# Moving the elementwise work of three attentions from GpSimd to VectorE in a two-layer hybrid encoder

## The chip, the cores and the metric

The kernel runs on one core of a Trainium2 chip, in one launch. The metric is the device time of an execution in microseconds; of several executions the median is given. A core has five engines with queues of their own: TensorE (PE, its weight loads PEld), VectorE (DVE), ScalarE (ACT), GpSimd (POOL) and SyncE (SP, which issues the DMAs here). Each works its queue off in order; they wait for each other by semaphores.

## The reference

Two layers (`DEPTH`), 512 tokens, 1024 features, all in float32. In each layer a wide projection feeds three attentions of 8 heads whose gated outputs are added:

```python
h = rms_norm(x, norm_mix[l]);  u = h @ w_in[l]
qa, ka, va, fa, qd, kvd, kr, qc, kc, vc, gl = split(u)
# A: causal, with cumulated log forget gates; q and k normalised per head
ya = prefix_block_attention(rms_norm(qa), rms_norm(ka), va, True, cum_logf)
# B: low rank; q and k of 64 normalised and 32 normalised and rotated columns a head
qb  = rms_norm(qd, mla_q_norm[l]) @ w_q_up[l]
kvb = rms_norm(kvd, mla_kv_norm[l]) @ w_kv_up[l]
q_mla = concat([rms_norm(qb[..., :64]), rope(rms_norm(qb[..., 64:]))])
k_mla = concat([rms_norm(kvb[..., :64]), rope(rms_norm(kr))])
yb = prefix_block_attention(q_mla, k_mla, kvb[..., 64:], False)
# C: chunks, with a clipped relative bias; q and k normalised per head
yc = chunk_band_attention(rms_norm(qc), rms_norm(kc), vc, rel_bias[l])
x = x + sum(sigmoid(gl + b_gate) * (y_n @ w_branch[l, n]) for n in A, B, C) @ w_out[l]
x = x + relu(rms_norm(x, norm_ffn[l]) @ w_ff1[l])**2 @ w_ff2[l]
```

## The kernel before

Every float32 product is made of three matmuls of the rounded form `fp32r`: each operand is split in a high and a low part, and high x high, low x high and high x low are added in PSUM. A weight chunk of 1024 columns comes by DMA into `raw`; ScalarE rounds it to `whi` (L140), VectorE subtracts to get `wlo` (L141). There are three buffers of each, and `take` puts both splits some places ahead of where it is called. Of each step of three matmuls it is the third that reads `wlo`.

The order of TensorE's instructions is written by the program (`manual_schedule` names PE alone). On the other engines a scheduler orders the instructions from their dependencies and priorities, so the order there follows when the data would be ready; what is moved from one engine to another also moves its neighbours.

A layer runs so: `qk_proj` projects A's queries and keys (four token blocks of 128) and normalises them per head: squares and means in `evac`, a reciprocal root by Newton steps (`rsqrt`, L251 to L255), the factor `fqk`, and eight multiplies (L403) over both `tok` tiles. `rotary_key` (L496 to L517) normalises and rotates the shared key. `attention` is a generator that is run step by step between the matmuls of other work (`fill`): scores S, transposed probabilities P (`ptl`, L715), values V, where every second head ends with the scale of the pair (L736), and transposes T of the next heads. Then C in the same way, with `branch(0)` as filler, and then B.

For B a string of letters (`TUNE["mla"]`) sets the order of the matmuls: `d` and `u` are the down projections (`mla_down`, whose evacuation splits the result, L456 and L457, squares it, L459, and adds the squares, L461), `0` and `1` the sums of these squares on TensorE and the factors from them (`mla_factor`: `ps_sum`, L292, then L480 to L483), `q` the queries' up projection (`mla_q`), `k` that of keys and values (`mla_kv`, weights `kvup`), `b` steps of `branch(2)`, `t` the transposes that attention B begins with (`ps_q`, L584), `g` a gate:

```python
mla='ddddddddddddubuubu0qqqbbqqqqqbbuuuubqbbb1kbbktkkkbbbkkkbtbbgg',
```

`mla_q` ends with the norms and rotations of the four token blocks (L568 to L576: six multiplies and adds each), two blocks on VectorE and two on GpSimd:

```python
e = nc.gpsimd if t % 2 else nc.vector
```

`mla_kv` scales the keys in the same way (L541), after `mf`, the factor from `1`, has scaled the projection out of PSUM (L490, L492). `branch` multiplies each gate with the product (L810) and adds it to the merged output (L811), on GpSimd but in the last branch. GpSimd also adds the causal mask (L685), cumulates squares for the layer norms (L284), makes the rotary tables (L235) and copies the rotary key (L530).

Of the kernel before, what the change touches and what calls it, by code (L numbers as in the profile page):

```python
# [13 lines left out]
ALU = mybir.AluOpType  # L14
# [10 lines left out]
H = 8  # L25
HD = 64
NOPE = 64
ROPE = 32
# [44 lines left out]
    head=1.0,  # L73
# [103 lines left out]
class Kern:  # L177
# [201 lines left out]
    def qk_proj(self, l, col, scale, out, tags=("s", "s", "mm", "mm")):  # L379
        nc = self.nc  # L380
        tok = [self.tk("tok", [P, 2, 512], F32) for _ in range(2)]
        out.append(tok)
        ms = self.small(NT * H, "ms", 1)
        ms4 = ms.rearrange("p (t h) -> p t h", h=H)

        def evac(t, ps):
            u = tok[t // 2][:, t % 2]
            nc.scalar.activation(out=u, in_=ps, func=AF.Copy, scale=self.rtok[:, t : t + 1])
            sq = self.tmp()
            nc.scalar.activation(out=sq, in_=ps, func=AF.Square, scale=self.rtok[:, t : t + 1])  # L390
            nc.vector.tensor_reduce(out=ms4[:, t], in_=sq.rearrange("p (h d) -> p h d", d=HD), axis=AX.X, op=ALU.add)

        yield from self.win_group(l, col, evac, tags)
        v = self.small(NT * H, "msv", 1)
        nc.vector.tensor_scalar(out=v, in0=ms, scalar1=1.0 / HD, scalar2=EPS, op0=ALU.mult, op1=ALU.add)
        y = self.rsqrt(v, NT * H)
        f = self.small(NT * H, "fqk")
        nc.vector.tensor_scalar(out=f, in0=y, scalar1=scale, scalar2=None, op0=ALU.mult)
        f4 = f.rearrange("p (t h) -> p t h", h=H)
        for p in range(4):  # L400
            for tp in range(2):
                u = tok[tp][:, :, p * P : (p + 1) * P].rearrange("p t (h d) -> p t h d", d=HD)
                nc.gpsimd.tensor_tensor(out=u, in0=u, in1=f4[:, 2 * tp : 2 * tp + 2, 2 * p : 2 * p + 2].unsqueeze(3).to_broadcast([P, 2, 2, HD]), op=ALU.mult)  # L403

    def v_evac(self, vt, t, ps, sc):
        nc = self.nc
# [89 lines left out]
    def rotary_key(self):  # L496

        nc = self.nc
        ps = self.pt.tile([P, T], F32, tag="pt", name="ps_kr")
        for t in range(NT):  # L500
            nc.tensor.transpose(ps[:, t * ROPE : (t + 1) * ROPE], self.kr[:, t * P : (t + 1) * P], self.ident[0:ROPE, 0:ROPE])
        krt = self.sm.tile([P, NT, ROPE], F32, tag="krt", name="krt", bufs=1)
        nc.vector.tensor_tensor(out=krt, in0=ps[:, 0 : NT * ROPE].rearrange("p (t d) -> p t d", d=ROPE), in1=self.rtok.unsqueeze(2).to_broadcast([P, NT, ROPE]), op=ALU.mult)
        sq = self.tmp()[:, 0 : NT * ROPE].rearrange("p (t d) -> p t d", d=ROPE)
        nc.gpsimd.tensor_tensor(out=sq, in0=krt, in1=krt, op=ALU.mult)
        v = self.small(NT, "krv", 1)
        nc.vector.tensor_reduce(out=v, in_=sq, axis=AX.X, op=ALU.add)
        nc.vector.tensor_scalar(out=v, in0=v, scalar1=1.0 / ROPE, scalar2=EPS, op0=ALU.mult, op1=ALU.add)
        y = self.rsqrt(v, NT)
        tab, hr = self.rtab, ROPE // 2  # L510
        nc.gpsimd.tensor_tensor(out=krt, in0=krt, in1=y.unsqueeze(2).to_broadcast([P, NT, ROPE]), op=ALU.mult)
        sw = self.tmp()[:, 0 : NT * ROPE].rearrange("p (t d) -> p t d", d=ROPE)
        for c in range(2):
            nc.gpsimd.tensor_tensor(out=sw[:, :, c * hr : (c + 1) * hr], in0=krt[:, :, (1 - c) * hr : (2 - c) * hr], in1=tab[:, 3, :, c * hr : (c + 1) * hr], op=ALU.mult)
        nc.gpsimd.tensor_tensor(out=krt, in0=krt, in1=tab[:, 2], op=ALU.mult)
        nc.gpsimd.tensor_tensor(out=krt, in0=krt, in1=sw, op=ALU.add)
        self.krt = krt  # L517

    def mla_kv(self, l, state):
# [17 lines left out]
        for t in range(NT):  # L537
            tp, tt = divmod(t, 2)
            u = kt[tp][:, tt, :, 0:NOPE]
            e = nc.gpsimd if t % 2 else nc.vector  # L540
            e.tensor_tensor(out=u, in0=u, in1=y4[:, t].unsqueeze(2).to_broadcast([P, H, NOPE]), op=ALU.mult)  # L541
        yield from group(1, lambda t, ps: self.v_evac(vt, t, ps, f))

    def mla_q(self, l, state):
# [18 lines left out]
        tab, hr = self.rtab, ROPE // 2  # L563
        for t in range(NT):
            tp, tt = divmod(t, 2)
            e = nc.gpsimd if t % 2 else nc.vector
            u = qt[tp][:, tt, :, 0:NOPE]
            e.tensor_tensor(out=u, in0=u, in1=fq4[:, t, 0].unsqueeze(2).to_broadcast([P, H, NOPE]), op=ALU.mult)  # L568
            u = qt[tp][:, tt, :, NOPE:KB]
# [53 lines left out]
    def attention(self, l, branch, fill_ns, qkv):  # L623
# [94 lines left out]
        def values(h, gi, x):  # L718
# [14 lines left out]
            r0 = HD * (h % 2)  # L733
            nc.vector.tensor_tensor(out=y[r0 : r0 + HD], in0=yps[0:HD], in1=half[0:HD], op=ALU.add)
            if h % 2 == 1:
                (nc.gpsimd if h + 1 < H else nc.vector).tensor_tensor(out=y, in0=y, in1=head[h]["scale"], op=ALU.mult)  # L736
                a, b = self.ypool.tile([P, T], F32R, tag="yh", name="yh", bufs=4), self.ypool.tile([P, T], F32R, tag="yl", name="yl", bufs=4)
                nc.scalar.activation(out=a, in_=y, func=AF.Copy)
                nc.vector.tensor_tensor(out=b, in0=y, in1=a.bitcast(F32), op=ALU.subtract)
# [44 lines left out]
    def branch(self, l, n, y, done=None, pool=None):  # L784

        nc = self.nc
        for m in range(0, KT, 2):
# [10 lines left out]
            for u, k in order:  # L798
# [5 lines left out]
                if k == 3:  # L804
# [326 lines left out]
```

## Time and profile before

| what | value |
|---|---|
| median of 3 executions | 1841.53 us (1840.97 to 1844.39) |
| the profiled execution, its own time | 1842.65 us |
| its span, first to last instruction | 1840.9 us |
| mean granted TensorE clock | 0.996 |
| TensorE busy | 1808.0 us, 98% |
| VectorE busy | 1056.5 us, 57% |
| ScalarE busy | 784.6 us, 43% |
| GpSimd busy | 216.7 us, 12% (257 instructions) |

A row of a timeline gives the start in the span, the time taken, the engine, line and operation, what it writes and reads by the program's names, the shapes, and in brackets the idle time before it and what ended that. A matmul's end is modelled, so its length overlaps the next one's: matmuls of 512 columns start 0.23 us apart at full clock and are given 0.39 each. A wait of TensorE's is therefore read from the starts. Lengths on the other engines are measured, also with a small overlap of neighbours that do not depend on each other.

### The profile page before, as it was taken

The numbers are of one execution on the slowest core, as the hardware profiler recorded it, in microseconds if no ns is written. First come the engines' busy times: TensorE is split into PE (matmuls) and PEld (weight loads), VectorE is DVE, ScalarE is ACT, GpSimd is POOL, SyncE is SP. The second block draws the span as 40 slices with busy tenths as digits, with TensorE's granted clock in tenths as the row PEclk, the third lists the DMA queues.
The fourth block names the chain that finished last, engine by engine and source line by source line (L and its number), as shares of the span: only waits on it lengthen the run. The fifth ranks groups of instructions, "written<-read, shape, count | busy, mean of one in ns | idle before, by whom it ended". The sixth has DMA issues, their size and how long they took to land.

```text
span 1840.9 us, 23250 instructions
## 1 busy us (share of the span) xinstructions
PE 1808.0 (98%) x8496; PEld 1489.7 (81%) x8496; DVE 1056.5 (57%) x1994; ACT 784.6 (43%) x1369; POOL 216.7 (12%) x257
## 2 busy tenths in 40 slices
PE   8999999989999999999999999999899999999999
PEld 6888888868888888888888788888688888888887
DVE  7565477497765632553355654765977655325531
ACT  6565456446643222222245644664366432212311
POOL 1321200150011000000123202001500110000000
PEclk9999999999999999999999999999999999999999
DMA  5564365322353333333345633653234433333331
GB/s 179 157 167 122 104 182 143 121 94 87 114 167 92 94 101 92 93 102 109 109 125 144 172 109 108 185 146 118 86 92 141 135 92 103 93 92 97 97 115 58
DMA packets 84226, 217.85 MB, mean 118 GB/s; under 512 B 13696, under 2 KB 16768, under 8 KB 84112
## 3 DMA queue, kind: packets, MB, share of 16 engines
q1 hardware_dynamic: 84112, 216.37, 40.3%
q8 instruction: 67, 1.10, 0.2%
q14 instruction: 47, 0.39, 0.1%
HBM read 178.44 MB, written 12.71 MB: 104 GB/s over the span
## 4 chain that ended last, share of the span: by engine, by line
PE 87%; DVE 6%; ACT 3%; DMA 2%; issue 1%; SPq 1%; POOL 0%; DVEq 0%; ACTq 0%; POOLq 0%
PE ps L332 38%; PE ps_f L332 14%; PE ps_t L367 14%; PE ps_o L332 5%; PE ps_b L802 5%; PE ps_s L682 3%; PE ps_y L725 3%; PE ps_p L712 2%; PE ps_q L584 1%; DVE wlo L141 1%; SPq L599 1%; ACT whi L140 1%; DMA kl<-nat 1%; DMA cb<-cum 0%; PE ps_k L349 0%
## 5 line engine op out<-in xcount | busy, mean ns | idle before, releaser
L140 ACT ACTIVATE whi<-raw 128x1024 fp32r<-128x1024 f32 (+1 forms) x337 | 307.3, 919 | 771.8 <-issue 316.0
L141 DVE TENSOR_TENSOR wlo<-raw,whi 128x1024 fp32r<-128x1024 f32 (+1 forms) x337 | 358.9, 1069 | 253.2 <-ACT whi L140 237.6
L332 PE MATMUL ps<-ah,wlo 128*128 128x512 f32 x512 | 201.7, 394 | 0.0
L332 PE MATMUL ps<-ah,whi 128*128 128x512 f32 x512 | 201.7, 394 | 0.0
L332 PE MATMUL ps<-al,whi 128*128 128x512 f32 x512 | 201.7, 394 | 0.0
L332 PE MATMUL ps<-xgh,whi 128*128 128x512 f32 x512 | 199.4, 390 | 0.0
L332 PE MATMUL ps<-xgl,whi 128*128 128x512 f32 x512 | 199.2, 389 | 0.0
L332 PE MATMUL ps<-xgh,wlo 128*128 128x512 f32 x512 | 199.2, 389 | 0.0
L332 PE MATMUL ps_f<-xgh,whi 128*128 128x512 f32 x464 | 195.9, 422 | 0.0
L332 PE MATMUL ps_f<-xgh,wlo 128*128 128x512 f32 x464 | 182.5, 393 | 0.0
L332 PE MATMUL ps_f<-xgl,whi 128*128 128x512 f32 x464 | 182.1, 393 | 0.0
L367 PE MATMUL ps_t<-whi,xgh 128*128 128x512 f32 x384 | 151.4, 394 | 6.7 <-ACT whi L140 6.7
L367 PE MATMUL ps_t<-whi,xgl 128*128 128x512 f32 x384 | 150.2, 391 | 0.0
L367 PE MATMUL ps_t<-wlo,xgh 128*128 128x512 f32 x384 | 150.2, 391 | 0.0
L332 PEld LDWEIGHTS ps<-al,whi 128*128 128x128 f32 x512 | 95.7, 187 | 23.7
L332 PEld LDWEIGHTS ps<-ah,wlo 128*128 128x128 f32 x512 | 95.7, 187 | 23.7
L332 PEld LDWEIGHTS ps<-ah,whi 128*128 128x128 f32 x512 | 95.7, 187 | 23.7
L332 PEld LDWEIGHTS ps<-xgh,wlo 128*128 128x128 f32 x512 | 96.1, 188 | 20.1
L332 PEld LDWEIGHTS ps<-xgl,whi 128*128 128x128 f32 x512 | 96.1, 188 | 20.0
L332 PEld LDWEIGHTS ps<-xgh,whi 128*128 128x128 f32 x512 | 96.1, 188 | 19.9
L715 DVE TENSOR_TENSOR ptl<-ps_p,pth 128x512 fp32r<-128x512 f32 x144 | 85.9, 599 | 43.7 <-ACT pth L714 42.6
L956 DVE SCALAR_TENSOR_TENSOR t<-ps,rb 128x512 f32<-128x512 f32 x64 | 43.9, 691 | 114.2 <-PE ps L332 111.6
(196 smaller groups left out, 3202.8 us busy)
## 6 DMA issues: line engine op xcount, KB each, us to landing
raw<-w SPq DMA_DIRECT2D x277, 512.0 KB
qq<-nat SPq DMA_DIRECT2D x64, 128.0 KB
kk<-nat SPq DMA_DIRECT2D x64, 128.0 KB
kl<-nat SPq DMA_DIRECT2D x64, 128.0 KB
gd<-t SPq DMA_DIRECT2D x32, 256.0 KB
t<-rows SPq DMA_DIRECT2D x48, 128.0 KB
cb<-cum SPq DMA_DIRECT2D x16, 256.0 KB
cb<-gd SPq DMA_DIRECT2D x16, 256.0 KB
```

The lines of the kernel that those rows point to most:

```text
L140: nc.scalar.activation(out=hi[:, c : c + v], in_=raw[:, c : c + v], func=AF.Copy)
L141: nc.vector.tensor_tensor(out=lo[:, c : c + v], in0=raw[:, c : c + v], in1=hi[:, c : c + v].bitcast(F32), op=ALU.subtract)
L332: nc.tensor.matmul(out=ps, lhsT=a[:, k], rhs=b[k], start=first and k == 0 and j == 0, stop=last and k == n - 1 and j == 2)
L367: nc.tensor.matmul(out=pss[t][:, 0:width], lhsT=a[k][:, t * P : t * P + P], rhs=b[:, i], start=c == 0 and i == 0 and j == 0, stop=last and ...
L584: nc.tensor.transpose(ps[0:rows, t * P : (t + 1) * P], src(t), self.ident)
L599: nc.sync.dma_start(out=s[rows, u].bitcast(F32), in_=x[own].bitcast(F32))
L682: nc.tensor.matmul(out=ps[:, 0:n], lhsT=a[:, i * P : (i + 1) * P], rhs=b[:, 0:n], start=j == 0, stop=j == len(terms) - 1)
L712: nc.tensor.transpose(ps[:, o + (i - kb) * P : o + (i - kb + 1) * P], pr[:, offs[i] + kb * P : offs[i] + (kb + 1) * P], self.ident)
L715: nc.vector.tensor_tensor(out=pl[:, 0:w], in0=ps[:, 0:w], in1=ph[:, 0:w].bitcast(F32), op=ALU.subtract)
L725: nc.tensor.matmul(out=yps[:, kb * P : T], lhsT=qkv[2][kb // 2][:, kb % 2, h, :], rhs=head[h][gi][x][:, o : o + T - kb * P], start=gi == 0 ...
L802: nc.tensor.matmul(out=pss[u], lhsT=chunk[a][:, u, k], rhs=y[b][k], start=k == 0 and j == 0, stop=k == 3 and j == 2)
L956: nc.vector.scalar_tensor_tensor(out=t, in0=ps, scalar=0.0, in1=self.rb, op0=ALU.max, op1=ALU.mult)
```

## The change

Seven places in the attentions and in `branch` issue on VectorE what GpSimd did: the norms (L403), the rotary key (L505 to L516), the odd token blocks of B's keys (L541) and queries (L568 to L576), the scale of a pair (L736) and the addition of a gated product (L811). In the changed kernel lines behind 540 count one less.

```diff
-                nc.gpsimd.tensor_tensor(out=u, in0=u, in1=f4[:, 2 * tp : 2 * tp + 2, 2 * p : 2 * p + 2]
...
+                nc.vector.tensor_tensor(out=u, in0=u, in1=f4[:, 2 * tp : 2 * tp + 2, 2 * p : 2 * p + 2]
...
-        nc.gpsimd.tensor_tensor(out=sq, in0=krt, in1=krt, op=ALU.mult)
+        nc.vector.tensor_tensor(out=sq, in0=krt, in1=krt, op=ALU.mult)
...
-        nc.gpsimd.tensor_tensor(out=krt, in0=krt, in1=sw, op=ALU.add)
+        nc.vector.tensor_tensor(out=krt, in0=krt, in1=sw, op=ALU.add)
...
-            e = nc.gpsimd if t % 2 else nc.vector
-            e.tensor_tensor(out=u, in0=u, in1=y4[:, t].unsqueeze(2).to_broadcast([P, H, NOPE]), op=ALU.mult)
+            nc.vector.tensor_tensor(out=u, in0=u, in1=y4[:, t].unsqueeze(2).to_broadcast([P, H, NOPE]), op=ALU.mult)
...
-            e = nc.gpsimd if t % 2 else nc.vector
+            e = nc.vector
...
-                (nc.gpsimd if h + 1 < H else nc.vector).tensor_tensor(out=y, in0=y, in1=head[h]["scale"], op=ALU.mult)
+                nc.vector.tensor_tensor(out=y, in0=y, in1=head[h]["scale"], op=ALU.mult)
...
-                        (nc.vector if done else nc.gpsimd).tensor_tensor(out=s, in0=s, in1=g, op=ALU.add)
+                        nc.vector.tensor_tensor(out=s, in0=s, in1=g, op=ALU.add)
```

The order on TensorE is the same. GpSimd keeps 48 rows in its queue's listing, which had 130. On VectorE the order changes at each of the places. The first one is in layer 0, in branch B, at the end of `mla_q`: VectorE's queue from the split of the last down projection (L457; `st`) over the sum of its squares (L461; `pr`) to the mean behind the sums (L480). Before:

```order
L457 SCALAR_TENSOR_TENSOR st<-ps_f,vec,st 128x512
L575 TENSOR_TENSOR tok<-tok,rtab 128x8x32
L573 TENSOR_TENSOR t_3957<-tok,rtab 128x8x16
L576 TENSOR_TENSOR tok<-tok,t_3943 128x8x32
L461 TENSOR_TENSOR pr<-pr 128x512
L573 TENSOR_TENSOR t_3957<-tok,rtab 128x8x16
L141 TENSOR_TENSOR wlo<-raw,whi 128x1024
L575 TENSOR_TENSOR tok<-tok,rtab 128x8x32
L810 SCALAR_TENSOR_TENSOR cb<-cb,ps_b 128x512
L480 SCALAR_TENSOR_TENSOR mv_4005<-ps_sum,r_4006 128x4
```

The L141 in it splits the first weights of `kvup`. In the changed kernel (lines one less, so L575 is L574 there):

```order
L457 SCALAR_TENSOR_TENSOR st<-ps_f,vec,st 128x512
L572 TENSOR_TENSOR t_3943<-tok,rtab 128x8x16
L569 TENSOR_TENSOR tok<-tok,fqv 128x8x32
L574 TENSOR_TENSOR tok<-tok,rtab 128x8x32
L461 TENSOR_TENSOR pr<-pr 128x512
L575 TENSOR_TENSOR tok<-tok,t_3943 128x8x32
L572 TENSOR_TENSOR t_3950<-tok,rtab 128x8x16 x2
L567 TENSOR_TENSOR tok<-tok,fqv 128x8x64
L574 TENSOR_TENSOR tok<-tok,rtab 128x8x32
L569 TENSOR_TENSOR tok<-tok,fqv 128x8x32
L480 SCALAR_TENSOR_TENSOR mv_4005<-ps_sum,r_4006 128x4
```

Four rotations stand ahead of L457 now (L567, L569, L567, L572) where six stood, and L141 is no longer between L461 and L480. It stands behind nine more rotations and the small steps of the factor:

```order
L575 TENSOR_TENSOR tok<-tok,t_3957 128x8x32
L254 SCALAR_TENSOR_TENSOR rs_t_4012<-rs_t_4012,mv_4005 128x4
L572 TENSOR_TENSOR t_3964<-tok,rtab 128x8x16
L255 SCALAR_TENSOR_TENSOR rs_y_4011<-rs_t_4012,rs_y_4011 128x4
L572 TENSOR_TENSOR t_3964<-tok,rtab 128x8x16
L253 TENSOR_TENSOR rs_t_4012<-rs_y_4011 128x4
L141 TENSOR_TENSOR wlo<-raw,whi 128x1024
L254 SCALAR_TENSOR_TENSOR rs_t_4012<-rs_t_4012,mv_4005 128x4
L574 TENSOR_TENSOR tok<-tok,rtab 128x8x32
L255 SCALAR_TENSOR_TENSOR rs_y_4011<-rs_t_4012,rs_y_4011 128x4
L809 SCALAR_TENSOR_TENSOR cb<-cb,ps_b 128x512
L483 TENSOR_TENSOR mf_4007<-rs_y_4011,rtok 128x4
```

Of the 24 rotations 22 are ahead of this L141; the factor `mf` (L483) comes soon behind it.

The second place is in attention A of layer 0, where the first pair of heads ends: VectorE's queue from the value sum (L734) to the low part of the output (L739; L738 in the changed kernel). Before:

```order
L734 TENSOR_TENSOR t_1017<-ps_y,t_1163 64x512
L691 ISA pr,mn<-ps_s,cb 128x512
L691 ISA mn 128x1
L715 TENSOR_TENSOR ptl<-ps_p,pth 128x512
L739 TENSOR_TENSOR yl<-t_1017,yh 128x512
```

In the changed kernel:

```order
L733 TENSOR_TENSOR t_1017<-ps_y,t_1163 64x512
L690 ISA pr,mn<-ps_s,cb 128x512
L690 ISA mn 128x1
L735 TENSOR_TENSOR t_1017<-t_1017,t_1105 128x512
L714 TENSOR_TENSOR ptl<-ps_p,pth 128x512
L690 ISA pr,mn<-ps_s,cb 128x384
L690 ISA mn 128x1
L738 TENSOR_TENSOR yl<-t_1017,yh 128x512
```

The scale of the pair (L736, here L735) now stands in VectorE's queue ahead of the low part of the probabilities.

## Rows read from the trace of the kernel before

**Rows 1.** The page, busy time by engine: us, share of the span, instructions.

```profile
PE 1808.0 (98%) x8496; PEld 1489.7 (81%) x8496; DVE 1056.5 (57%) x1994; ACT 784.6 (43%) x1369; POOL 216.7 (12%) x257
```

**Rows 2.** TensorE's waits: waited for; us in total, times, longest us.

```profile
PE ps_sum L292 <- DVE pr L461: 7.8, 2, 3.9
...
PE ps_q L584 <- DVE tok L541: 2.2, 3, 1.0
```

**Rows 3.** Timeline of TensorE at the first wait for the sums.

```profile
381.79 0.40 PE L802 MATMUL ps_b<-yh,wlo 128*128 128x512 f32 x1
386.10 1.87 PE L292 MATMUL ps_sum<-ones,pr 128*128 128x2 f32 x8 [3.91 <-DVE pr L461]
387.83 1.20 PE L367 MATMUL ps_t<-whi,st 128*128 128x512 f32 x2
388.83 0.63 PE L367 MATMUL ps_t<-wlo,st 128*128 128x512 f32 x1
```

**Rows 4.** Stretches: us, busy time of PE, PEld, DVE, ACT, POOL, then granted clock.

```profile
382.00:386.00 4.00, 0.19 (x1) 0.00 (x0) 4.00 (x7) 1.54 (x2) 3.77 (x7) 0.98 0.00 0
386.00:393.00 7.00, 6.90 (x21) 5.79 (x22) 7.00 (x12) 0.00 (x0) 5.26 (x4) 0.52 0.40 113
...
1300.50:1307.50 7.00, 7.00 (x21) 5.71 (x21) 7.00 (x11) 0.00 (x0) 5.27 (x4) 0.51 0.39 114
```

**Rows 5.** Timeline of VectorE in the same place.

```profile
377.27 0.69 DVE L568 TENSOR_TENSOR tok<-tok,fqv 128x512 f32<-128x512 f32 x1
377.88 1.27 DVE L570 TENSOR_TENSOR tok<-tok,fqv 128x256 f32<-128x256 f32 x1
...
382.36 0.74 DVE L457 SCALAR_TENSOR_TENSOR st<-ps_f,vec,st 128x512 fp32r<-128x512 f32 x1
...
385.10 0.94 DVE L461 TENSOR_TENSOR pr<-pr 128x512 f32<-128x512 f32 x1
...
386.70 1.21 DVE L141 TENSOR_TENSOR wlo<-raw,whi 128x1024 fp32r<-128x1024 f32 x1
...
389.37 0.41 DVE L576 TENSOR_TENSOR tok<-tok,t 128x256 f32<-128x256 f32 x1
389.71 1.24 DVE L481 TENSOR_SCALAR mv<-mv 128x4 f32<-128x4 f32 x1
```

**Rows 6.** Timelines of GpSimd (two rows) and ScalarE there.

```profile
377.37 1.50 POOL L568 TENSOR_TENSOR tok<-tok,fqv 128x512 f32<-128x512 f32 x1 [2.75 <-DVE fqv L562]
...
389.46 1.46 POOL L811 TENSOR_TENSOR mg<-mg,cb 128x512 f32<-128x512 f32 x1 [0.96 <-DVE mv L480]
...
383.13 0.60 ACT L459 ACTIVATE pr<-ps_f 128x512 f32<-128x512 f32 x1 [5.10 <-DVE st L457]
```

**Rows 7.** Groups of VectorE's instructions: busy us, mean ns of one, idle before.

```profile
L573 DVE TENSOR_TENSOR t<-tok,rtab 128x128 f32<-128x128 f32 x8 | 6.7, 862 | 0.0
...
L736 DVE TENSOR_TENSOR t<-t,t 128x512 f32<-128x512 f32 x6 | 4.2, 693 | 0.2
...
L507 DVE TENSOR_REDUCE krv<-t 128x4 f32<-128x128 f32 x2 | 0.6, 280 | 0.4 <-POOL t L505 0.4
```

**Rows 8.** Timeline of TensorE, the waits behind the first.

```profile
399.65 0.73 PE L367 MATMUL ps_t<-whi,st 128*128 128x512 f32 x2 [0.59 <-ACT t L492]
...
412.63 0.42 PE L584 MATMUL ps_q<-ident,tok 128*96 128x128 f32 x2 [1.03 <-DVE tok L541]
...
415.81 0.73 PE L682 MATMUL ps_s<-st 96*128 96x512 f32 x2 [1.14 <-DVE st L587]
...
421.90 1.30 PE L682 MATMUL ps_s<-st 96*128 96x512 f32 x3 [0.52 <-DVE mn L691]
```

**Rows 9.** Timeline of VectorE: a pair's end in attention A; a projection of C.

```profile
134.66 0.69 DVE L715 TENSOR_TENSOR ptl<-ps_p,pth 128x512 fp32r<-128x512 f32 x1 [1.04 <-ACT pth L714]
...
205.59 1.23 DVE L141 TENSOR_TENSOR wlo<-raw,whi 128x1024 fp32r<-128x1024 f32 x1 [3.91 <-ACT whi L140]
```

More of the change, by code (lines that the diff above doesn't have):

```diff
@@ L402, in qk_proj @@
                 u = tok[tp][:, :, p * P : (p + 1) * P].rearrange("p t (h d) -> p t h d", d=HD)
-                nc.gpsimd.tensor_tensor(out=u, in0=u, in1=f4[:, 2 * tp : 2 * tp + 2, 2 * p : 2 * p + 2].unsqueeze(3).to_broadcast([P, 2, 2, HD]), op=ALU.mult)
+                nc.vector.tensor_tensor(out=u, in0=u, in1=f4[:, 2 * tp : 2 * tp + 2, 2 * p : 2 * p + 2].unsqueeze(3).to_broadcast([P, 2, 2, HD]), op=ALU.mult)
     def v_evac(self, vt, t, ps, sc):
@@ L510, in rotary_key @@
         tab, hr = self.rtab, ROPE // 2
-        nc.gpsimd.tensor_tensor(out=krt, in0=krt, in1=y.unsqueeze(2).to_broadcast([P, NT, ROPE]), op=ALU.mult)
+        nc.vector.tensor_tensor(out=krt, in0=krt, in1=y.unsqueeze(2).to_broadcast([P, NT, ROPE]), op=ALU.mult)
         sw = self.tmp()[:, 0 : NT * ROPE].rearrange("p (t d) -> p t d", d=ROPE)
         for c in range(2):
-            nc.gpsimd.tensor_tensor(out=sw[:, :, c * hr : (c + 1) * hr], in0=krt[:, :, (1 - c) * hr : (2 - c) * hr], in1=tab[:, 3, :, c * hr : (c + 1) * hr], op=ALU.mult)
-        nc.gpsimd.tensor_tensor(out=krt, in0=krt, in1=tab[:, 2], op=ALU.mult)
-        nc.gpsimd.tensor_tensor(out=krt, in0=krt, in1=sw, op=ALU.add)
+            nc.vector.tensor_tensor(out=sw[:, :, c * hr : (c + 1) * hr], in0=krt[:, :, (1 - c) * hr : (2 - c) * hr], in1=tab[:, 3, :, c * hr : (c + 1) * hr], op=ALU.mult)
+        nc.vector.tensor_tensor(out=krt, in0=krt, in1=tab[:, 2], op=ALU.mult)
+        nc.vector.tensor_tensor(out=krt, in0=krt, in1=sw, op=ALU.add)
         self.krt = krt
```

## The prediction

> **What bounds the kernel now.** I read the busy times first: TensorE is busy for 98% of the span and VectorE for 57% [rows 1]. The change touches no matmul and no matmul's place, so it can move the time only through TensorE's waits, and the second view is the list of those. It is short. Waiting for the sums of squares of the latent keys (`ps_sum`, released by VectorE's L461) takes 7.8 us in two pieces, one in each layer, and waiting for the scaled keys of branch B (L541) 2.2 us in three [rows 2]. The third view is TensorE in order of time at the first of these: its last matmul of `ps_b` starts at 381.79, the eight sums only at 386.10, and the projection `kvup` behind them at 387.83 [rows 3]. The fourth, the stretches with the granted clock, tells what such an idle time costs on top: in 386 to 393 the clock is 0.52 of full, so the 1.2 GHz level held for 0.48 x 7 / 0.5 = 6.7 us, until 392.7; at 1300.5 to 1307.5, in the other layer, it is 0.51 [rows 4]. The fifth shows why VectorE is late there: it runs the rotations of branch B's queries without a pause, and at the same time GpSimd runs the other half of them [rows 5, 6].
>
> These two do not run side by side. L568 of VectorE begins at 377.27 and takes 0.69, L568 of GpSimd begins at 377.37; VectorE's next multiply, on half the elements, takes 1.27 and ends at 379.15, some 0.29 after GpSimd's L568 has let go at 378.87. The same 128x256 size takes 0.41 at 389.37, when GpSimd is idle. L481, which works on four elements a partition, takes 1.24 at 389.71, while GpSimd adds a gate (L811, 1.46 from 389.46) [rows 5, 6]. So a GpSimd operation on two operands holds up a VectorE one that falls into it for nearly its whole length.
>
> **The change, part by part.** Everything is counted per layer; there are two.
>
> *Durations after the move.* 128x512 on VectorE takes 0.69 (L736, six of which are there already), 128x256 takes 0.41 [rows 5, 7]. For 128x128 no free multiply is in the trace; the bounds are the reduction L507 with 0.28 and the contended L573 with 0.86 [rows 7]. I take 0.28, since the two other sizes went back to such values where GpSimd was idle. Independent neighbours overlap by some 0.08 (377.27 + 0.69 against 377.88), so the steps are 0.61, 0.34 and 0.20.
>
> *Rotations (L568 to L576).* VectorE issues 24 instead of 12. Ahead of the split of `kvup`'s weights stand 22 of them now: 4 of 0.61, 10 of 0.34 and 8 of 0.20, 7.4 us together. With 0.86 - 0.28 = 0.58 more for each, as L573 has it, they would take 7.4 + 22 x 0.58 = 20.2, the other bound. The Trainium skill ("SBUF — State Buffer", Who interferes with whom) has it that a VectorE instruction with two SBUF inputs and a GpSimd instruction that reads SBUF exclude each other, whichever starts first. By that rule the free lengths hold once GpSimd has nothing here, as the trace suggests, and the sum stands; by the lengths as they are in the rows it would be the slow rival below. The added gate (L811, 0.61) goes ahead of the reciprocal roots, and one root step that was held for 1.1 is free again, so the first rotation starts at about 376.7 instead of 377.27. In the new order L457 comes behind four rotations (378.5, in place of 382.36) and L461 behind three more. ScalarE's square between them takes 0.60 and starts as L457 ends [rows 6], so L461 runs from 380.0 to 380.7. TensorE comes to the sums at 381.79 + 0.23 = 382.02: **the first wait is gone**, with 1.3 us to spare.
>
> *What is late next.* The eight sums take 0.8, the first two matmuls of `kvup` (which read `whi`) follow at 382.83, and the third reads `wlo`. Its split (L141) was in VectorE's queue behind L461 and one rotation; now it comes behind L461, fifteen rotations and ten small steps of the factor. From 380.6 that is 0.34 + 0.40 + 0.61 + 0.34 + 0.34 to 382.6, the mean (L480) when the sums are in at 383.0, then 3.7 us of rotations and small steps to 386.7, and 1.22 for the split. It ends at 387.9; before, it ended at 386.70 + 1.21 = 387.91 [rows 5]. By coincidence that is the same moment. So TensorE stands from 383.5 to about 387.95, 4.5 us, now at the third matmul of `kvup`, and the wait has changed its place. That third matmul starts 0.86 earlier than at 388.83 [rows 3]. An idle of that size cost the clock before, and I expect the fall again; coming back at 392.7 to 394, it leaves between 0.5 gained and 0.1 lost at the end of this stretch. I take **0.2**.
>
> *The waits behind it.* The factor `mf` (L483) was late because GpSimd's gates held three root steps for 1.1 us each; now it comes at 389.0, and TensorE's wait at 399.65 (idle 0.59; a start-to-start step of 0.23 under a modelled length of 0.39 makes each wait 0.16 longer than its idle) goes: **0.75**. The keys' scales (L541) are four of 0.61 on VectorE where two ran on each engine, but with the factor 9 us earlier they begin as soon as the keys are there, at about 406, and are through at 408.6, while TensorE, with its clock down, is at their transposes at about 410. That wait goes: 2.2 / 2 + 2 x 0.16 = **1.4**. The next one, for the split L587 (415.81, idle 1.14, so 1.3), shrinks to about 0.5, since the queue ahead of L587 stays the same: **0.8**. The one at 421.90 (0.52 + 0.16) goes, since a split held by GpSimd's gate ahead of the scores is free: **0.7** [rows 2, 8].
>
> *Norms (L403, 8 per projection, 64 in all).* They cost VectorE 8 x 0.34 = 2.7 us at each of eight places. VectorE idles 3.9 us between two splits there [rows 9], and with three weight buffers the split behind them is for a chunk that TensorE reads some 5 us later (24 matmuls of 0.23 to a chunk). Nothing, unless that slack is used up; then up to 2.7 a place.
>
> *Scales of the pairs (L736, 18), rotary key, remaining gates (L811).* 18 x 0.61 on VectorE in the softmax stream, ahead of L715. VectorE waits 1.04 for ScalarE at that very point in the second pair [rows 9]: nothing, at most 0.6 each where it does not wait.
>
> **Sum:** 0.2 + 0.75 + 1.4 + 0.8 + 0.7 = 3.85 per layer, 7.7 in all. The profiled execution took 1842.65 (span 1840.9 and 1.75 around it) and would take 1834.95; it stands 1.1 over the median of 1841.53, so the forecast is **1833.8**.
>
> **Rivals.** *The clock stays up.* The idle is now broken by sums and two matmuls. For: the stretch without matmuls of 512 columns shrinks from 5.8 us (382.0 to 387.83) to 4.5. Against: both layers fell, and 4.5 is still long. From 387.95 to 392.7 half of the time comes back, 2.4 in place of 0.2: 1831.6 if in one layer, 1829.4 if in both.
>
> *The long durations are the rotations' own* (broadcast and strided operands), not GpSimd's doing. Then the 22 take 12.8 us longer per layer ahead of the split, TensorE's third matmul comes 12 us later than now, and the later waits stay: about 1841.5 + 24 = 1865. It turns slower once the 22 take over 7.4 + 4.5 us, 0.54 each. Against it stand the 0.41 at 389.37 and the four elements that took 1.24. The Trainium skill ("Perfetto Trace Analysis", Optimizing Scalar/DVE Operations) says that it may pay to move work off a saturated VectorE, even to GpSimd, and that this might not help because they share a port. VectorE is saturated here (4.00 of 4.00 us in 382 to 386 [rows 4]), so the first half of that sentence speaks against the change; the trace bears out the second half.
>
> *The softmax stream pays.* If L736 delays L715 in all of the 18 places, 18 x 0.61 = 11 comes back: 1844.8; in half of them 1839.3. For: TensorE waits in the attentions are all on VectorE and ScalarE. Against: the pause of 1.04.
>
> **How the numbers follow.** Forecast 0.55, clock up in one layer or both 0.25, softmax stream 0.13, own durations or another loss on VectorE 0.07. About 0.2%, 3.7 us, is what a measurement can tell: faster 0.80, same 0.13, slower 0.07. The range goes from a little under the case of full clock in both layers, 1827.5, to 1840.5 in the softmax case.
>
> **What would show it.** Right: no wait at `ps_sum`, a wait of 4 to 5 us at `ps_t` on `wlo` (L141) in each layer, the granted clock near 0.5 for some 6 us behind it, L568 to L576 at 0.69, 0.41 and 0.28, and no wait on the keys' scales. Wrong: L461 still late, rotations over 0.5 on average, or new waits on `ptl` in the attentions.

## The result and the profile after

The changed kernel took **1831.96 us** (median of 6 runs, 1829.80 to 1833.69), the kernel before 1842.05 (6 runs, 1840.89 to 1844.70): a ratio of 0.9943, with an interval of 0.993 to 0.9955. That is 10.1 us, more than the 3.7 that a measurement can tell, 1.8 below the forecast of 1833.8 and inside its range. The profiled executions differ by as much: 1842.65 and 1832.57, spans 1840.9 and 1830.8.

The page's busy times, us, share and instructions (before: [rows 1]):

```profile
PE 1803.2 (98%) x8496; PEld 1489.0 (81%) x8496; DVE 1080.6 (59%) x2132; ACT 783.8 (43%) x1369; POOL 88.8 (5%) x119
```

138 instructions went over. GpSimd lost 127.9 us by it and VectorE gained 24.1, 0.17 for each, less than the shortest of them takes (0.24, the 128x64 multiplies of the rotary key): VectorE's own instructions have become shorter. TensorE's waits (waited for; us, times, longest) [rows 2]:

```profile
PE ps_t L367 <- DVE wlo L141: 8.4, 2, 4.2
...
PE ps_s L681 <- DMA kl<-nat: 3.9, 4, 1.0
PE ps_y L724 <- DVE ptl L714: 1.2, 2, 1.1
...
PE ps_s L681 <- DVE st L586: 0.6, 2, 0.3
```

The sums (`ps_sum`) and the keys (`tok`, L540) are gone from the list; in their place stands one wait a layer for the split of `kvup`'s weights, as foretold. The wait on `ptl` is new; a new wait there was named as a sign of being wrong. Its long piece (1.06) is in attention C of layer 0: VectorE stands 1.08 there for a load of C's queries (`qq`, from 285.88 to 286.96), and its split of `ptl` comes behind. It is not the scale of a pair that holds it. The waits for the loads of `kl` are the same 3.9 in four as before. TensorE in order of time, at the places of [rows 3, 8]:

```profile
382.31 0.40 PE L801 MATMUL ps_b<-yh,wlo 128*128 128x512 f32 x1
382.55 0.95 PE L292 MATMUL ps_sum<-ones,pr 128*128 128x2 f32 x8
383.36 0.71 PE L367 MATMUL ps_t<-whi,st 128*128 128x512 f32 x2
388.29 0.80 PE L367 MATMUL ps_t<-wlo,st 128*128 128x512 f32 x1 [4.22 <-DVE wlo L141]
...
398.81 0.62 PE L367 MATMUL ps_t<-whi,st 128*128 128x512 f32 x2
...
409.91 0.60 PE L583 MATMUL ps_q<-ident,tok 128*96 128x128 f32 x4
```

The sums follow the last matmul of `ps_b` by 0.24 us where it was 4.31. In the windows (us; busy PE, PEld, DVE, ACT, POOL; granted clock; DMA) the idle time still costs the clock, in both layers [rows 4]:

```profile
382.00:386.00 4.00, 2.07 (x14) 1.49 (x12) 3.61 (x16) 0.00 (x0) 0.00 (x0) 1.00 0.00 0
386.00:393.00 7.00, 4.71 (x11) 3.79 (x12) 7.00 (x20) 1.27 (x2) 0.00 (x0) 0.51 0.42 114
...
1294.00:1301.00 7.00, 4.49 (x11) 3.55 (x12) 7.00 (x20) 1.27 (x2) 0.00 (x0) 0.51 0.42 112
```

VectorE there, to be held against [rows 5]: the 128x256 multiply behind the first L567 takes 0.42 and not 1.27, and L481 on four elements 0.17 and not 1.24.

```profile
377.17 0.69 DVE L567 TENSOR_TENSOR tok<-tok,fqv 128x512 f32<-128x512 f32 x1
377.78 0.42 DVE L569 TENSOR_TENSOR tok<-tok,fqv 128x256 f32<-128x256 f32 x1
...
380.45 0.69 DVE L461 TENSOR_TENSOR pr<-pr 128x512 f32<-128x512 f32 x1
...
383.94 0.17 DVE L481 TENSOR_SCALAR mv<-mv 128x4 f32<-128x4 f32 x1
...
387.00 1.23 DVE L141 TENSOR_TENSOR wlo<-raw,whi 128x1024 fp32r<-128x1024 f32 x1
```

By groups (busy us, mean ns, idle before) the durations are those taken in the prediction, the 128x128 multiply's among them, for which only bounds were to be had [rows 7]:

```profile
L567 DVE TENSOR_TENSOR tok<-tok,fqv 128x512 f32<-128x512 f32 x8 | 5.5, 688 | 0.1
...
L572 DVE TENSOR_TENSOR t<-tok,rtab 128x128 f32<-128x128 f32 x16 | 4.4, 286 | 0.0
...
L569 DVE TENSOR_TENSOR tok<-tok,fqv 128x256 f32<-128x256 f32 x8 | 3.4, 421 | 0.0
```

Where the 10.2 us between the last matmuls come from, by the starts of the same matmul in both traces:

| us gained | layer 0 | layer 1 | forecast |
|---|---|---|---|
| sums, split and clock | 0.61 | 0.84 | 0.2 |
| factor (L492) | 0.87 | 0.74 | 0.75 |
| keys' scales (L541) | 1.54 | 1.49 | 1.4 |
| split of the latent keys (L587) | 1.15 | 1.17 | 0.8 |
| last scores (421.90) | 0.56 | 0.52 | 0.7 |
| **branch B** | **4.73** | **4.76** | **3.85** |
| attention A | 0.45 | 0.82 | 0 |
| attention C | -0.76 | 0.27 | 0 |

The program's start takes 0.21 back, and 0.14 lies between the places. Branch B is the result. A second profile of the same changed kernel (after_again, the last experiment) gives 4.60 and 4.04 for it: the first line is 0.51 and 0.25 there, and the others agree within 0.13. So the first line varies by up to 0.6 from one execution to the next. In the attentions these two profiles differ by up to 1.5 us in a stretch, so a sum of that size is not resolved there by one profile of each; single waits are (rest_back below). The -0.76 holds the wait behind the load of C's queries; of the other runs best1 alone shows it, with 1.08.

### The profile page after: what moved, and what is told of

It is laid out like the page before. It is cut to its first block, busy times and chain, and to the rows that moved or that the text cites. A ratio compares the mean times of both kernels' runs of the same rounds, so it can differ in the third digit from the quotient of the medians.

```text
span 1830.8 us, 23198 instructions
## 1 busy us (share of the span) xinstructions
PE 1803.2 (98%) x8496; PEld 1489.0 (81%) x8496; DVE 1080.6 (59%) x2132; ACT 783.8 (43%) x1369; POOL 88.8 (5%) x119
## 4 chain that ended last, share of the span: by engine, by line
PE 94%; DVE 2%; DMA 1%; ACT 1%; SPq 1%; issue 0%; POOL 0%; DVEq 0%; ACTq 0%; POOLq 0%
PE ps L332 39%; PE ps_f L332 17%; PE ps_t L367 16%; PE ps_b L801 7%; PE ps_o L332 5%; PE ps_s L681 4%; PE ps_y L724 3%; PE ps_p L711 3%; PE ps_q L583 1%; SPq L598 1%; DMA kl<-nat 1%; PE ps_k L349 0%; PE ps_sum L292 0%; DMA qq<-nat 0%; ACT whi L140 0%
## 5 line engine op out<-in xcount | busy, mean ns | idle before, releaser
L141 DVE TENSOR_TENSOR wlo<-raw,whi 128x1024 fp32r<-128x1024 f32 (+1 forms) x337 | 353.6, 1053 | 236.0 <-ACT whi L140 220.4
```

What stands on the lines that cost most here:

```text
L141: nc.vector.tensor_tensor(out=lo[:, c : c + v], in0=raw[:, c : c + v], in1=hi[:, c : c + v].bitcast(F32), op=ALU.subtract)
```

## Experiments: undoing one part

Each of these four is the changed kernel with one part of the work on GpSimd again; the fifth is the kernel before with one part moved. "Cost" is how much longer branch B is than in the changed kernel's trace, layer 0 / layer 1. The kernel before took 1843.04 beside these and beside the three that follow them, 1843.43 beside spare and best1, and 1842.37 beside both and after_again.

**rot_back**, half of the rotations on GpSimd again:

```diff
-            e = nc.vector
+            e = nc.gpsimd if t % 2 else nc.vector
```

> The changed kernel with the odd token blocks' rotations (L567 to L575) on GpSimd again, 12 a layer; all else stays on VectorE. My theory (a GpSimd operation with two operands holds VectorE up for its length): VectorE's rotations beside them take 1.27 and 0.86 again in place of 0.42 and 0.28, the latent keys' squares are summed some 5 us later (L461 near 386), TensorE waits 3 to 4 us at the sums in each layer and then once more, 1 to 3 us, at the third matmul of kvup: 2 to 4 us a layer slower than the changed kernel, 1836 to 1840. Rival (the two engines run side by side, GpSimd was only slow and late itself): VectorE has 4 us less to do ahead of the split of kvup, its durations stay at 0.69, 0.42 and 0.28, the wait at kvup goes: about 1822.

Measured: 1836.23 (ratio 0.9957, 0.9944 to 0.9969), cost 1.85 / 3.06. VectorE is held again, and TensorE, in the second fence, waits for the sums:

```profile
375.24 1.27 DVE L569 TENSOR_TENSOR tok<-tok,fqv 128x256 f32<-128x256 f32 x1
376.43 1.10 DVE L567 TENSOR_TENSOR tok<-tok,fqv 128x512 f32<-128x512 f32 x1
377.45 1.13 DVE L572 TENSOR_TENSOR t<-tok,rtab 128x128 f32<-128x128 f32 x1
...
385.08 0.15 DVE L480 SCALAR_TENSOR_TENSOR mv<-ps_sum,r 128x4 f32<-128x4 f32 x1
...
395.11 0.16 DVE L483 TENSOR_TENSOR mf<-rs_y,rtok 128x4 f32<-128x4 f32 x1
```

```profile
382.28 1.86 PE L292 MATMUL ps_sum<-ones,pr 128*128 128x2 f32 x8 [2.11 <-DVE pr L461]
...
397.70 0.73 PE L367 MATMUL ps_t<-whi,st 128*128 128x512 f32 x2 [2.12 <-ACT t L492]
```

The wait for the sums is 2.1, less than before: no addition of GpSimd's holds L251 ahead of the rotations (0.19 here, 1.28 before), and L457 stands behind four of VectorE's rotations and not six. The one for the factor (L492) is 2.12 where it was 0.59 [rows 8]. Both come with the rotations, but the cost does not stand at the sums. Up to the end of the lower clock behind them this run is 0.85 and 1.15 us ahead of the changed kernel, since the wait at the third matmul of `kvup` is gone in layer 0 and 1.3 in layer 1; it loses 2.4 and 4.0 at the factor (in layer 1 the clock falls once more behind it, to 0.50 from 1307.4 to 1310.7). From L480 to L483 it takes 10.03 us here, and no step of the root is longer than 0.17: other work of VectorE's stands between them. Before it took 8.84, in the changed kernel 5.68. So the order of the queue, which the move changes too, makes most of this wait, and not a hold of the root steps.

**gate_back**, the gated additions on GpSimd again but for the last branch's:

```diff
-                        nc.vector.tensor_tensor(out=s, in0=s, in1=g, op=ALU.add)
+                        (nc.vector if done else nc.gpsimd).tensor_tensor(out=s, in0=s, in1=g, op=ALU.add)
```

> The changed kernel with the addition of the gated products (L810) on GpSimd again, 16 places. My theory: an addition of 1.46 there holds small steps of the reciprocal root and splits on VectorE for about 1.1 each, so the factor comes later, the waits at the second evacuation of the keys (0.75) and in the first scores (0.7) come back in each layer, and the split that the third matmul of kvup waits for ends up to 1 us later: 1.5 to 4 us slower than the changed kernel, 1833.5 to 1836. Rival (all of the gain is the rotations'): within 1 us of the changed kernel, 1832.

Measured: 1834.41 (0.9949, 0.9935 to 0.9962), cost 1.85 / 1.27. Timelines of GpSimd, VectorE and TensorE:

```profile
402.94 1.29 POOL L810 TENSOR_TENSOR mg<-mg,cb 128x512 f32<-128x512 f32 x1 [7.57 <-DVE cb L809]
```

```profile
387.96 1.25 DVE L483 TENSOR_TENSOR mf<-rs_y,rtok 128x4 f32<-128x4 f32 x1
...
403.00 1.28 DVE L254 SCALAR_TENSOR_TENSOR rs_t<-rs_t,fkk 128x32 f32<-128x32 f32 x1
```

```profile
412.21 0.74 PE L681 MATMUL ps_s<-st 96*128 96x512 f32 x2 [1.16 <-DVE st L586]
```

The addition of a gate, 1.29, holds the keys' root step L254 from 403.00 to 404.28, its whole length; in the changed kernel that step takes 0.19, and in the kernel before it was held in the same way:

```profile
406.53 1.28 DVE L254 SCALAR_TENSOR_TENSOR rs_t<-rs_t,fkk 128x32 f32<-128x32 f32 x1
```

The scales and the split L586 behind it come late, and the wait of 1.14 [rows 8] is back with 1.16. Of the cost 1.17 and 1.23 stand here; the rest is in the stretch of the sums and the lower clock, where two profiles of one kernel differ by up to 0.6. The waits for the factor and at the last scores did not come back, though L483 was held too.

**key_back**, the odd blocks' scales (L540) on GpSimd again:

```diff
-            nc.vector.tensor_tensor(out=u, ...
+            (nc.gpsimd if t % 2 else nc.vector).tensor_tensor(out=u, ...
```

> The changed kernel with the odd token blocks' key scales (L540) on GpSimd again, 2 a layer. By the prediction's step the wait there went because the factor comes earlier, not because VectorE does all four: the keys' scales are ready before TensorE comes to the transposes, no wait or at most 0.5 us, 1832 to 1833. Rival (the wait went because VectorE does them): the wait of 1.4 us a layer comes back, 1834.8.

Measured: 1831.36 (0.993, 0.9917 to 0.9942), cost -0.09 / 0.38: nothing. The keys' transposes find their operands ready either way, once what stands ahead of them is no longer late.

**rest_back**, the norms (L403), the rotary key (L505 to L516) and the scales of the pairs (L735) on GpSimd again:

```diff
-                nc.vector.tensor_tensor(out=u, in0=u, in1=f4[...
+                nc.gpsimd.tensor_tensor(out=u, in0=u, in1=f4[...
...
-                nc.vector.tensor_tensor(out=y, in0=y, in1=head[h]["scale"], op=ALU.mult)
+                (nc.gpsimd if h + 1 < H else nc.vector).tensor_tensor(out=y, in0=y, in1=head[h]["scale"], op=ALU.mult)
```

> The changed kernel with the norms (L403), the rotary key (L505 to L516) and the scales of the pairs (L735) on GpSimd again: the parts that the prediction costs at nothing. By it the time stays within 1 us of the changed kernel, 1831 to 1833, with the waits of 0.1 to 0.7 us in the attentions that the changed kernel lost coming back at a few places. Rival (the softmax stream pays for the scales on VectorE, the norms delay the splits behind them): faster than the changed kernel by 2 to 6 us, 1826 to 1830.

Measured: 1834.19 (0.9948, 0.9936 to 0.996), 1.2 over the expected range; cost in B 0.60 / -0.17; the attentions are some 0.5 us longer in all than in the first profile of the changed kernel and some 4.5 longer than in its second. The rival that has the softmax stream pay falls: giving the work back to GpSimd made nothing faster. A small gain of the move can be read from single waits. TensorE in attention A of layer 0, in the kernel before and in this run:

```profile
141.13 0.39 PE L725 MATMUL ps_y<-pth,v 128*128 128x256 f32 x1 [0.50 <-ACT pth L714]
```

```profile
141.84 0.38 PE L724 MATMUL ps_y<-pth,v 128*128 128x256 f32 x1 [0.50 <-ACT pth L713]
```

Layer 1 has the same wait, and the changed kernel's list has it in neither. By the starts this matmul gains 0.5, and another of `ps_y` some 24 us ahead of it 0.4, in each layer and in all ten profiles with this work on VectorE; in rest_back and rot_only, which have it on GpSimd, they gain nothing (0.2 once). So the part is worth about 0.9 us a layer in attention A. Which of norms, rotary key and pairs brings it is not shown.

**rot_only**, the kernel before with the rotations alone moved:

```diff
-            e = nc.gpsimd if t % 2 else nc.vector
+            e = nc.vector
```

> The kernel before with nothing but the rotations (L568 to L576) moved to VectorE. My theory: they carry the first wait's end and with it most of the factor's earlier time, the gates' additions 2.4 and the rest 1 to 2, by the runs that undid them: 1835.5 (1834 to 1838). Rival (the parts only pay together, since a GpSimd addition still holds the root steps): 1839 to 1842. Rival on the other side (the rotations are all of it): 1832.

Measured: 1833.99 (0.9955, 0.9942 to 0.9969), B 1.37 / 0.29 longer than in the changed kernel. This is at the lower edge of the expected range. By the medians the rotations alone bring 9.05 us. Of the waits of the kernel before, its list has none for the sums, the factor, the keys or the last scores; for the split it has 8.6 in two, and for the scores' operands (L587) 2.0 in four. The four costs of undoing add up to 8.75 of the 9.49 that branch B gained; but rotations moved by themselves bring 7.83 of it, and undone by themselves take back 4.91, so the parts do not simply add: with the rotations the order of the whole queue moves (rot_back). What rot_only lacks in both layers is the split L587, 0.8 each; the rest of its 1.37 and 0.29 is the stretch of the sums and the lower clock.

## Experiments: what holds VectorE

**micro** is a small program of its own that computes none of the outputs. VectorE runs the same set of operations four times over: alone, and beside an unbroken row of GpSimd instructions, once with two operands in SBUF, once with one, once with none:

```diff
+    for _ in range(48):
+        nc.gpsimd.tensor_tensor(out=q, in0=c, in1=d, op=ALU.mult)
...
+    for _ in range(48):
+        nc.gpsimd.tensor_scalar(out=q, in0=c, scalar1=2.0, scalar2=None, op0=ALU.mult)
...
+    for _ in range(64):
+        nc.gpsimd.memset(q, 1.0)
```

> A small program of its own that computes none of the outputs: VectorE runs four each of multiplies of two SBUF operands (128x512, 128x256, 128x128), of PSUM by SBUF, of one operand by a constant (128x512, 128x4), and sums (128x512), first alone, then while GpSimd runs multiplies of two operands, then of one operand by a constant, then fills that read nothing. My theory: alone 0.6 to 0.7, 0.35 to 0.42 and 0.2 to 0.28; beside GpSimd's multiplies of two operands each VectorE instruction with two SBUF operands, and those of one operand by a constant, wait for the end of a GpSimd operation (some 1.3 to 1.5 each in all), the sums and the one with PSUM do not. Beside GpSimd's multiplies by a constant the same if any reading operation of GpSimd holds VectorE up, free if it takes two operands on GpSimd. Rival (VectorE is slowed for some other reason at that place of the kernel, such as its operands' strides): the lengths are the free ones in all four parts.

Groups by line (busy us, mean ns, idle before). L123 to L135 run alone, L142 to L154 beside L139, L161 to L173 beside L158, L180 to L192 beside the fills:

```profile
L158 POOL TENSOR_SCALAR q<-c 128x512 f32<-128x512 f32 x48 | 72.4, 1509 | 3.9
L139 POOL TENSOR_TENSOR q<-c,d 128x512 f32<-128x512 f32 x48 | 62.4, 1300 | 3.7
...
L142 DVE TENSOR_TENSOR o<-a,b 128x512 f32<-128x512 f32 x4 | 6.5, 1632 | 0.1
L144 DVE TENSOR_TENSOR o<-a,b 128x256 f32<-128x256 f32 x4 | 5.5, 1366 | 0.1
L150 DVE TENSOR_SCALAR o<-a 128x512 f32<-128x512 f32 x4 | 5.3, 1336 | 0.1
L146 DVE TENSOR_TENSOR o<-a,b 128x128 f32<-128x128 f32 x4 | 5.2, 1288 | 0.1
...
L161 DVE TENSOR_TENSOR o<-a,b 128x512 f32<-128x512 f32 x4 | 3.1, 764 | 0.1
L123 DVE TENSOR_TENSOR o<-a,b 128x512 f32<-128x512 f32 x4 | 3.1, 763 | 0.1
...
L148 DVE TENSOR_TENSOR o<-ps,b 128x512 f32<-128x512 f32 x4 | 2.8, 691 | 0.1
L152 DVE TENSOR_REDUCE o<-a 128x8 f32<-128x512 f32 x4 | 2.7, 686 | 0.1
...
L169 DVE TENSOR_SCALAR o<-a 128x512 f32<-128x512 f32 x4 | 2.7, 685 | 0.1
...
L163 DVE TENSOR_TENSOR o<-a,b 128x256 f32<-128x256 f32 x4 | 2.3, 569 | 0.1
...
L131 DVE TENSOR_SCALAR o<-a 128x512 f32<-128x512 f32 x4 | 1.7, 426 | 0.1
L125 DVE TENSOR_TENSOR o<-a,b 128x256 f32<-128x256 f32 x4 | 1.7, 426 | 0.1
...
L165 DVE TENSOR_TENSOR o<-a,b 128x128 f32<-128x128 f32 x4 | 1.5, 364 | 0.1
L127 DVE TENSOR_TENSOR o<-a,b 128x128 f32<-128x128 f32 x4 | 1.2, 293 | 0.1
```

Beside two-operand GpSimd instructions a 128x128 multiply takes 1288 ns in place of 293 and a 128x256 one 1366 in place of 426: about GpSimd's own 1300, whatever the size. With an operand in PSUM (L148) or in a sum (L152) nothing changes. Beside GpSimd's multiplies by a constant, which read one operand, the 128x512 multiply keeps its length, 764 against 763, though each of those lasts 1509; the smaller ones are not wholly free (569 for 426, 364 for 293), nor is VectorE's multiply by a constant (685 for 426). Beside the fills the two-operand multiplies take 692, 426 and 293, as alone or less, and the multiply by a constant 677.

## Experiments: the wait that is left, and its clock

**early** gives VectorE the split of `kvup`'s first weights earlier, by a higher priority for that one `take`:

```diff
-        with k.tc.high_priority(k.ahead):
+        with k.tc.high_priority(ahead or k.ahead):
...
-            hi, lo = self.streams[l].take(width * len(kk), *key)
+            hi, lo = self.streams[l].take(width * len(kk), *key, ahead=60 if key == ("kvup", 0) else None)
```

> The changed kernel with the splits of kvup's first weights given a higher priority (60 places ahead instead of 30), which puts the L141 that the third matmul of kvup waits for ahead of L457 in VectorE's queue. If that wait of 4.4 us in each layer and the lower clock behind it (some 4.5 us at half rate, 2.2 lost) are the new bound of this stage, both go: 6.6 a layer, less a wait of about 1.4 at the queries' transposes, which then come before the last rotations: 1821.6 (1819 to 1825). Rival (the stage is bound by VectorE's sum of work, so that the wait moves on to the factor, the transposes or the next weights in full): 1828 to 1832.

Measured: 1830.66 (0.9937, 0.9924 to 0.9949), cost 0.50 / 0.46. Timeline and window:

```profile
388.42 0.79 PE L801 MATMUL ps_b<-yh,whi 128*128 128x512 f32 x1 [4.25 <-DVE cb L809]
```

```profile
388.00:394.00 6.00, 5.58 (x13) 4.42 (x14) 4.62 (x9) 1.56 (x3) 0.00 (x0) 0.50 0.33 87
```

The time is the rival's, not the forecast's 1821.6. The wait for the split, 4.22, is gone, and 4.25 stands behind the first six matmuls of `kvup`, for the gated product `cb` (L809) that frees a buffer of `ps_b`. It starts at 387.69 on VectorE, behind the same rotations. What came late was VectorE's queue; pulling one piece out of it hands the wait to the next.

**early_t** also puts the first transposes of attention B one step of the key projection later, so that they are not waited for:

```diff
-    mla='ddddddddddddubuubu0qqqbbqqqqqbbuuuubqbbb1kbbktkkkbbbkkkbtbbgg',
+    mla='ddddddddddddubuubu0qqqbbqqqqqbbuuuubqbbb1kbbkktkkbbbkkkbtbbgg',
```

> As the run before, and the first transposes of attention B (the queries') one step of the key projection later, by one letter of the string that orders TensorE: kt becomes kkt with the third k taken from behind. The wait of 1.4 at the transposes goes as well: 1819 (1816 to 1822). Rival: the transposes' split is then what the first scores wait for, no better than the run before.

Measured: 1830.87 (0.9941, 0.9929 to 0.9954), cost -0.68 / 0.18; the wait for `cb` is 8.5 in two, as in early. The forecast missed here too, and by the same step: the wait had only been handed on.

**spare** leaves the wait and fills it: 18 matmuls of 512 columns into a spare PSUM bank, which nothing reads, between the second and third matmul of `kvup`:

```diff
+    def spare(self, a, b):
+        ps = self.pt.tile([P, T], F32, tag="pt", name="ps_spare"); [self.nc.tensor.matmul(out=ps, lhsT=a, rhs=b, start=True, stop=True) for _ in range(18)]
```

> The changed kernel with 18 more matmuls of 512 columns between the second and the third matmul of kvup in each layer, into a PSUM bank that nobody reads: 18 x 0.23 = 4.1 us of work in the 4.4 us in which TensorE waits there for L141. If the lower clock behind that wait comes from the idle time, it stays at 2.4 GHz, and what the half rate took from 388.3 to 392.9 and from 1296.5 to 1300.9 comes back by half, 2.2 us a layer, less up to 1 a layer where TensorE now comes too early to the keys: 1827.5 to 1829.5 with more work done. Rival (the clock falls at this place for another reason, or what it costs is hidden behind VectorE anyway): 1832 or more.

Measured: 1827.45 (0.9915, 0.9901 to 0.9928), cost -1.91 / -1.81, at the lower end of what was expected. The windows of both layers show the full clock:

```profile
386.00:393.00 7.00, 6.91 (x32) 5.12 (x31) 6.88 (x13) 2.89 (x4) 0.00 (x0) 1.00 0.53 150
1294.00:1301.00 7.00, 7.00 (x34) 5.67 (x33) 6.88 (x11) 5.00 (x9) 0.00 (x0) 1.00 0.77 235
```

From the start of the sums to the third matmul of `kvup` it takes 5.74 us here (381.13 to 386.87) and in the changed kernel (382.55 to 388.29): the wait is the same, and the 1.8 to 1.9 us a layer are the clock's alone. Against the second profile of the changed kernel they are 2.0 and 2.5.

**best1** takes both chunks of `kvup` early, gives the gated products of `branch(2)` priority and puts the first transposes of attention B behind the next three steps of the branch:

```diff
-    mla='ddddddddddddubuubu0qqqbbqqqqqbbuuuubqbbb1kbbktkkkbbbkkkbtbbgg',
+    mla='ddddddddddddubuubu0qqqbbqqqqqbbuuuubqbbb1kbbkkkkbbbtkkkbtbbgg',
...
+            hi, lo = self.streams[l].take(width * len(kk), *key, ahead=60 if key[0] == "kvup" else None)
...
+                        with self.tc.high_priority(120 if n == 2 else 0):
```

> The changed kernel with three more steps so that no single one of VectorE's late results takes the place of the last: the splits of both kvup chunks 60 places ahead, the gated products of the branches (L809, here L810) 120 places ahead, since the run with only the first split moved waited 4.2 us for one of them, and the first transposes of attention B behind the next three steps of the branch. By the order and the lengths of the rows, TensorE then runs from the sums to the third chunk of the branch without a wait and stands some 3 us there for its split, which comes behind all of the rotations: the wait of 4.4 and the half rate (2.2) go, 3 come back, 3.6 a layer: 1824.8 (1821 to 1829). Rival (VectorE's sum of work from the queries' factor to the keys' scales bounds this stage whatever its order): the wait only moves again, 1829 to 1832.

Measured: 1827.61 (0.9912, 0.9898 to 0.9925), cost -1.27 / -0.99; within the expected range, 2.8 over its middle. The wait is down to 2.43, at the branch's last weights, and behind it the clock fell once more (0.72 in this window), which the expectation had not counted:

```profile
396.71 0.79 PE L801 MATMUL ps_b<-yh,wlo 128*128 128x512 f32 x1 [2.43 <-DVE wlo L141]
```

```profile
394.00:400.00 6.00, 3.57 (x10) 2.63 (x9) 5.82 (x10) 1.95 (x3) 0.00 (x0) 0.72 0.69 210
```

**both** is best1 with 11 unread matmuls in that wait:

```diff
+                    ... n == 2 and (m, u, k, j) == (6, 0, 0, 1) and self.spare(chunk[a][:, u, k], y[b][k])
```

> The run best1 with 11 more matmuls of 512 columns between the second and the third matmul of the branch's last weights, where best1 waited 2.4 us in each layer and ran at half rate behind it (clock 0.72 in 394 to 400): 11 x 0.23 = 2.5 us of work whose result nobody reads. The clock stays at 2.4 GHz and the 4 to 5 us at half rate cost half of that less: 2 to 2.5 a layer, less some 1 where the keys' scales are then late: 1823 to 1826. Rival (VectorE's queue bounds what follows, so that a faster TensorE only waits at the keys): 1827.5, as best1 and spare.

Measured: 1826.02 (0.9908, 0.9894 to 0.9921), cost -2.60 / -2.54, the lowest time of the study, though its interval overlaps those of spare and best1; the clock is 1.00 over the whole span, this window included:

```profile
394.00:400.00 6.00, 6.00 (x27) 4.64 (x26) 6.00 (x11) 2.08 (x3) 0.00 (x0) 1.00 0.68 210
```

**after_again** is the changed kernel once more, with no edit but an empty line (its lines from 540 on are numbered as in the kernel before):

> The changed kernel itself, beside the other run of this call on the same chip: 1830 to 1834, if the differences of 2 to 4 us between the runs of this study are the kernels' and not the chips'.

Measured: 1830.4 (0.9931, 0.9918 to 0.9945), B 0.12 / 0.70 longer than in its first profile. A cost under about 0.7 in branch B is therefore no finding, which holds for key_back, rest_back, early and early_t.

## Why the prediction was right

*GpSimd holds VectorE, and free lengths return.* Right. micro shows it apart from this kernel, and the groups after have 688, 421 and 286 ns. The rival of own durations falls with the same rows. The hold is enough for the first wait: from 377.27 to the end of L461 at 386.04, VectorE's ten rows of the kernel before take some 4.2 us more than the same shapes in the changed kernel (an estimate by these lengths), and TensorE's wait was 4.1. Of what the Trainium skill ("SBUF — State Buffer", Who interferes with whom) says, that a VectorE instruction with two SBUF inputs collides with a GpSimd instruction that reads SBUF, the traces bear out the case with two operands; beside one that reads a single operand the 128x512 multiply took 764 ns against 763 and the 128x256 one 569 against 426, and there the measurement decides.

*The first wait goes, one of 4.5 takes its place, the clock falls again.* Right in kind and place: TensorE stood 4.22 at the third matmul of `kvup` in both layers, with the clock at 0.51 behind it (for 4.65 us, not some 6). The rival of a clock that stays up did not come; spare prices it at 1.8 to 1.9 a layer. The term was **mis-sized**: 0.2 was taken, 0.61 and 0.84 measured in the first profile, 0.51 and 0.25 in the second. The third matmul came 1.06 earlier, not 0.86, measured from where TensorE stands ahead of the sums, which was 0.52 later than before; and by the same measure the half rate ended at 392.4 (392.94 in the trace), ahead of the 392.7 to 394 that were expected. The upper end of 0.5 would have been the better choice, but no single number fits: the low level (1.2 GHz) began 2.2 and 2.45 us ahead of the third matmul in the first profile and 1.9 and 0.8 ahead of it in the second, and only the part of it behind that matmul costs.

*Factor and keys.* 0.75 and 1.4 foretold, 0.74 to 0.87 and 1.49 to 1.54 measured. The cause given for the first, gates that held three root steps, stands in the rows of the kernel before (L481, L253 and L255 take 1.24 to 1.26), but the runs do not show that it decided: gate_back holds L483 for 1.25 and TensorE does not wait, while rot_back, where no step is held, brings the wait back with 2.1, and rot_only, with the gates still on GpSimd, removes it. In the kernel before the sums were late by 4.1 and the held steps added some 3.2, each more than the 0.75 of the wait; which of them made it is not separated. That the amount was right is in part luck. The keys go with the factor: key_back costs nothing, and rot_only, which leaves the scales on both engines, has no wait for them.

*The split L587.* **Mis-sized**: 0.8 taken, 1.15 and 1.17 measured (1.11 and 1.10 in the second profile). The step that failed is "the queue ahead of L587 stays the same". It did not: the keys' root step L254 was held there by a gate, which the prediction had not looked at, and gate_back brings 1.16 back.

*Last scores.* 0.7 foretold, 0.52 to 0.56 measured; the cause given, a split held by a gate, is not shown: no part undone brought this wait back, and gate_back and rot_only, with the gates on GpSimd, do not have it. The cause stays open, and the amount was near by luck.

*Norms, rotary key, pairs: nothing.* **Mis-sized** as well: the feared losses did not come, and two waits in attention A went, about 0.9 us a layer, by rest_back, rot_only and the other profiles. The reading behind it was not complete: TensorE's waits in the attentions are not all on VectorE and ScalarE, four of them, 3.9 in all, are for loads of `kl`, before and after.

*The sum.* 7.7 foretold, 9.49 in branch B by the first profile and 8.64 by the second; the 1.79 between, in the first, are two mis-sized terms (1.05 and 0.72 over both layers) and, with 0.02, the remainders of the others. That the attentions, the start and the rest add only 0.71 to it is chance: attention A gained 1.27, and the wait behind a load in C took 1.08 back. In the second profile, without that wait, the span is 12.3 shorter than before.

## What to carry to other kernels

Before giving a second engine half of the elementwise work, look for instructions of VectorE that are longer than their size elsewhere while GpSimd runs: here the shared half cost VectorE so much that taking it all back added only 0.17 us an instruction. Look also at how the move reorders the other engine's queue: in rot_back that, and no hold of a root step, made the largest loss. When a wait is removed, ask which result in the same queue is late next; only moving several at once shortened it. And where TensorE must wait some microseconds anyway, unread matmuls in the gap kept the clock up and were worth 1.8 to 1.9 us a place in spare and 1.3 to 1.55 in both (by one profile each).

## What the runs showed of the hardware

- Whether GpSimd's instruction has one or two operands decided, not how long it lasts: its multiply by a constant, 1509 ns, left VectorE's 128x512 multiply as it was (764 ns against 763), the two-operand one of 1300 ns doubled it (1632). VectorE's 128x256 multiply takes 426 ns alone, 569 beside the one and 1366 beside the other.
- The hold does not shrink with the work: four elements a partition (L483 in gate_back) took 1.25 us.
- VectorE's multiply by a constant takes 426 ns alone, 677 beside GpSimd's fills, 685 beside its multiplies by a constant and 1336 beside two-operand ones.
- A kernel that issues 36 matmuls more, all unread, is no slower, and by the medians 3 us faster, than the kernel without them (1827.45 against 1830.4 in after_again; the ratios' intervals, 0.9901 to 0.9928 and 0.9918 to 0.9945, still overlap). The 1.8 to 1.9 us a layer are read from the trace.
